# Transfers of the job's operands and sums issued by GpSimd instead of SyncE, in a hybrid decoder layer

## The chip, the cores and the metric

The kernel runs on one core of a Trainium2 chip. The metric is the device time of one launch in microseconds, lower is better. The engines are named as in the profile: PE (TensorE), DVE (VectorE), ACT (ScalarE), POOL (GpSimd) and SP (SyncE, which here only issues DMAs). Each works through its own queue in order, and an instruction that waits for a semaphore holds all that stand behind it on its engine. "SPq" in the profile is SP's queue.

## The reference

One decoder layer on x of 2048 positions by 1024 channels, all in float32:

```python
xn = rms_norm(h, ln_g)
proj = xn @ w_in                                   # 1024 -> 6144 columns
b_gate, c_gate, x_conv, g_conv, x_lru, g_lru = split(proj)
y_conv = headwise_rms_norm(b_gate * conv3(c_gate * x_conv)) * silu(g_conv)
y_lru = headwise_rms_norm(rg_lru(x_lru)) * silu(g_lru)
y = concatenate([y_conv, y_lru])                   # 2048 columns
out = rms_norm(h + y @ w_out, final_g)
```

`rg_lru` is a causal width-4 convolution, two block-diagonal gate maps with sigmoids, and a linear recurrence over the positions.

## The kernel before

Both large products run as a Strassen-Winograd scheme with seven products in place of eight. Each operand of a product is split into a high and a low float32r part, so that one product is three matmuls of 128x128 by 128x512 for each of four k blocks (`mm`, L886). One of the seven takes PE some 2.7 us.

The work is a list of 64 steps. 24 input steps for the first half of the positions (h = 0) and 24 for the second (h = 1) go in rounds of three, one round for each of the eight column blocks k: `lru` ("l"), `conv_a` ("a") and `conv_b` ("b"). 16 output steps ("o") follow. The program is written out in slots, one product each. `tick()` starts a slot: it runs what was put off with `at(slots, ...)` and then one piece of the generator `jobs()`. What a slot holds is the order of every engine's queue.

In the second half the weights' seven sums come ready from HBM (`sd`, loaded as `s<-sd` by `s_loads`, L218, seven 512 KB loads a step). SP issues such a load when PE has freed one of seven buffers.

From step 30 (h = 1, k = 2) on, `jobs()` prepares the left operand of the first six output blocks beside the input steps. One job, of which one runs in each round:

- `load_z` loads four tiles `raw` of y (from `yd`, L309) and their row factors `zr` (from `rsd`, L312 or L314 and L316) into the eight buffers of the pool `raw`. Where h = 0 each of the four `zr` tiles takes two DMAs, so a job has 12 loads, else 8. Jobs 1, 2, 5 and 6 have 12, jobs 3 and 4 have 8.
- two and three slots later DVE multiplies raw by zr, then adds and subtracts to get the seven sums (`s`, `raw`).
- for each sum ACT casts the high part (`so`, L417), DVE takes the low part, and `so` is stored (L422, 512 KB, seven for each job). Its tile is one of four of the tag "hl", which the high parts of the norms (`qh`, `ql`) and `st` use too.
- jobs 1 to 4 also take two blocks of `w_out` each: four loads `traw` (`blocks`, L381) into buffers that `zr` has left, four sums on DVE (`sums`, `more`), four stores `td` (L395).

All of these DMAs, and every other one but two, stand on SP, in the order of the program. That order also holds the stores `yd<-gl` and `yd<-gb` of each round's results (`finish`, L575), two for each, which read the tile g of `lru` or `conv_b`. These tiles share a tag with two buffers ("o2"), so the next round's first write to gl waits for the store of the one before last in that tag.

POOL makes in the second half the products g * sigmoid(g) (`silu`: gl and gb, 128x1024) and the two parts of the gate weights (`load_gate_w`: bh, bl), some 6 us a round. The DVE instruction L570 in `finish` reads these products. The kernel is built with `dynamic_dma_scratch_size=1024`; no DMA stands on POOL.

Of the kernel before, what the change touches and what calls it, by code (L numbers as in the profile page):

```python
# [17 lines left out]
P = 128  # L18
# [4 lines left out]
NB = C // P  # L23
# [15 lines left out]
def hymba_kernel(ctx: ExitStack, tc: tile.TileContext, x, xt, w_in, par, lamc, w_gate, w_out, final_g, out):  # L39
    nc = tc.nc  # L40
# [100 lines left out]
    def at(slots, *fs):  # L141
        if slots == 0:
            for f in fs:
                f()
        else:
            due.append([slots, fs])
# [150 lines left out]
    def load_z(h, m, zr, wait):  # L297
        r = [piece("raw") for _ in range(4)]
        fs = []
        for i in range(2):  # L300
            c, b = divmod(2 * m + i, NB)
            assert c < 2 or normed
            zz_, zq_ = [], []
            z2 = wt(("u", "r")[i], "zr") if zr else None
            for q in range(2):
                zz = r[2 * i + q].rearrange("p (k t) -> p k t", k=NB)
                zq = z2[:, q * C:(q + 1) * C] if zr else piece("zr")
                k0 = (1 - h) * KT + q * NB
                nc.sync.dma_start(zz, yd[c][b, :, k0:k0 + NB, :])  # L309
                zq = zq.rearrange("p (k t) -> p k t", k=NB)  # L310
                if h == 1:
                    nc.sync.dma_start(zq, rsd[c][b:b + 1, k0:k0 + NB, :].broadcast_to((P, NB, P)))  # L312
                else:
                    nc.sync.dma_start(zq[:64], rsd[c][b:b + 1, k0:k0 + NB, :].broadcast_to((64, NB, P)))  # L314
                    k0 += KT
                    nc.sync.dma_start(zq[64:], rsd[c][b:b + 1, k0:k0 + NB, :].broadcast_to((64, NB, P)))  # L316
                fs.append(lambda zz=zz, zq=zq: tt(zz, zz, zq, ALU.mult))
        if wait is not None:
            for i in range(2):
                at(max(wait + i, 1), *fs[2 * i:2 * i + 2])  # L320
        return r, fs
# [37 lines left out]
    def jobs():  # L359
        tjobs = [(t, j) for t in (2, 3) for j in range(NB)]  # L360
        for ph, m in ((0, 0), (0, 1), (1, 0), (1, 1), (0, 2), (0, 3)):
            (a11, a12, a21, a22), fs = load_z(ph, m, False, None)
            yield
            yield
            for f in fs[:2]:
                f()
            yield
            for f in fs[2:]:
                f()
            yield  # L370
            x_ = aux("s3")
            tt(x_, a11, a21, ALU.subtract)
            tt(a21, a21, a22, ALU.add)
            b = {}

            def blocks():
                if tjobs:
                    b[0] = tjobs.pop(0)
                    b[1] = [piece("traw") for _ in range(4)]
                    for p, src in zip(b[1], w_blocks(*b[0])):  # L380
                        nc.sync.dma_start(p, src)  # L381

            def sums():
                if b:
                    b11, b12, b21, b22 = b[1]
                    tt(b11, b12, b11, ALU.subtract)
                    tt(b12, b22, b12, ALU.subtract)

            def more():
                if b:  # L390
                    b11, b12, b21, b22 = b[1]
                    tt(b22, b22, b11, ALU.subtract)
                    tt(b21, b21, b22, ALU.subtract)
                    to = td[b[0]]
                    at(1, lambda: [nc.sync.dma_start(to[n], v) for n, v in enumerate((b22, b11, b12, b21))])  # L395
                    b.clear()

            blocks()
            prev = None
            nothing = lambda: None  # L400
            items = [(0, a11, lambda: tt(a11, a21, a11, ALU.subtract)), (3, x_, nothing), (2, a21, nothing),
                     (1, a11, nothing), (4, a12, lambda: tt(a12, a12, a11, ALU.subtract)),
                     (6, a22, nothing), (5, a12, nothing)]
            for n, (i, v, after) in enumerate(items):
                if prev:
                    prev()
                    prev = None
                if n in (1, 5):
                    sums()
                if n in (2, 6):  # L410
                    more()
                if n == 4:
                    blocks()
                while not may():
                    yield
                t, = hl_tile("so")
                nc.scalar.copy(t[:, 0:C], v)  # L417

                def prev(t=t, i=i, v=v, after=after, dst=so[ph, m]):
                    tt(t[:, C:2 * C], v, t[:, 0:C].bitcast(F32), ALU.subtract)  # L420
                    after()
                    at(2, lambda: nc.sync.dma_start(  # L422
                        dst[i], t.bitcast(F32).rearrange("p (h c) -> p h c", h=2)))
                    at(3, lambda: hl_done(1))

                yield
            prev()
            made.add((ph, m))
            yield
# [854 lines left out]
```

## Time and profile before

| | |
|---|---|
| median of three runs | 1422.15 us (1421.93 to 1424.15) |
| the profiled execution's own time | 1420.66 us |
| its span in the trace | 1418.5 us |
| granted TensorE clock, mean | 0.983 |
| DVE, ACT, POOL busy | 75%, 55%, 17% of the span |
| DMA, mean rate over the span | 262 GB/s |
| DMAs named by the change | 42 so stores of 512 KB, 32 traw loads and 32 td stores of 256 KB, first and last 682.7 and 1088.7 us (with the six jobs' loads) |

A line of the profile with a time in front gives start and length in us, the engine, the line of the kernel, the operation, "written tile <- read tiles", shapes, how many in a row, and in brackets how long the engine stood still just before and what ended that. A line of the waits gives the engine and what waited, for whom, then total us, how many, and the longest. A line of a group gives after the bar the busy total and the mean in ns, and then the idle time before. Lines with three numbers between slashes are least, median and most.

### The profile page before, as it was taken

To read this page: it belongs to the slowest core of one execution; us is meant where nothing else is said; L and a number is where in the kernel's file an instruction comes from. 1 tells how busy PE (TensorE), PEld (TensorE's weight loads), DVE (VectorE), ACT (ScalarE), POOL (GpSimd) and SP (SyncE) were. 2 spreads that over 40 slices of the span, in tenths; PEclk is the share of its full clock that TensorE was granted. 3 is DMA by queue.
4 is the path that set the end of the run, shared out by engine and by line. 5 is a ranking of instruction groups with operands and counts; after the bars stand their busy time and mean duration, and the time that the engine had idled before them with its cause. 6 is when DMAs were issued, how large, how long until landed. Compare 5 with 4: busy or idle time off the path is not lost.

```text
span 1418.5 us, 16980 instructions
## 1 busy us (share of the span) xinstructions
PE 1332.1 (94%) x5732; PEld 1069.0 (75%) x5732; DVE 1070.9 (75%) x1273; ACT 782.1 (55%) x1165; POOL 245.8 (17%) x159
## 2 busy tenths in 40 slices
PE   6889999999999997899998999999996999989997
PEld 5768777778777775677886878787875788867886
DVE  7689788898989889777767667665657648668885
ACT  7576757667656756475563645463647313334443
POOL 2104333433534330001000010101010000000000
PEclk9989999999999998999999999999998999999999
DMA  5037797998888865631899999998888998698643
GB/s 213 30 118 277 266 286 213 305 321 284 312 283 297 310 244 203 235 102 30 281 318 340 330 345 331 353 301 308 277 282 318 353 298 272 207 405 298 214 155 144
DMA packets 165190, 371.02 MB, mean 262 GB/s; under 512 B 17264, under 2 KB 52464, under 8 KB 165104
## 3 DMA queue, kind: packets, MB, share of 16 engines
q1 hardware_dynamic: 164816, 369.63, 76.3%
q8 instruction: 45, 0.74, 0.2%
q14 instruction: 41, 0.34, 0.1%
q10 hardware_dynamic: 288, 0.32, 0.1%
HBM read 224.45 MB, written 145.43 MB: 261 GB/s over the span
## 4 chain that ended last, share of the span: by engine, by line
PE 64%; DMA 12%; ACT 10%; DVE 8%; issue 3%; SPq 1%; POOL 0%; DVEq 0%; ACTq 0%
PE bank L886 61%; ACT i L673 2%; DMA traw<-in_w_out_dram 2%; ACT r L673 2%; PE norm_ps L559 2%; PE gate L666 2%; DVE s L160 2%; DMA zr<-rsd 2%; DMA raw<-yd 1%; DMA s<-so 1%; DVE traw L160 1%; DMA yd<-gl 1%; DVE tl L160 1%; DMA sd<-s 1%; DMA traw<-td 1%
## 5 line engine op out<-in xcount | busy, mean ns | idle before, releaser
L886 PE MATMUL bank<-th,s 128*128 128x512 f32 x3608 | 1143.7, 393 | 44.6 <-DMA s<-so 8.8
L886 PEld LDWEIGHTS bank<-th,s 128*128 128x128 f32 x3608 | 683.4, 189 | 206.4 <-issue 11.0
L886 PE MATMUL bank<-tl,s 128*128 128x512 f32 x1804 | 709.1, 393 | 7.5 <-DVE tl L160 7.3
L886 PEld LDWEIGHTS bank<-tl,s 128*128 128x128 f32 x1804 | 341.6, 189 | 82.5 <-DVE tl L160 11.6
L160 POOL TENSOR_TENSOR s<-raw,s 128x512 fp32r<-128x512 f32 x62 | 120.8, 1961 | 252.3 <-ACT s L197 177.3
L197 ACT CAST s<-raw 128x512 fp32r<-128x512 f32 x136 | 81.9, 616 | 58.9 <-PE bank L886 46.0
L1223 ACT COPY u<-bank 128x512 f32<-128x512 f32 x58 | 34.0, 586 | 139.1 <-PE bank L886 90.1
L160 DVE TENSOR_TENSOR tl<-traw,th 128x512 fp32r<-128x512 f32 x102 | 69.4, 706 | 48.8 <-ACT th L454 29.4
L160 DVE TENSOR_TENSOR s<-s,s 128x512 fp32r<-128x512 f32 x102 | 99.9, 980 | 5.4 <-ACT s L197 5.4
L160 POOL TENSOR_TENSOR gb<-gb,sg 128x1024 f32<-128x1024 f32 x16 | 42.2, 2634 | 352.0 <-ACT sg L599 259.5
L160 DVE TENSOR_TENSOR s<-raw,s 128x512 fp32r<-128x512 f32 (+1 forms) x120 | 93.4, 802 | 10.0 <-ACT s L197 5.3
L1220 ACT COPY q<-bank 128x512 f32<-128x512 f32 x58 | 33.8, 583 | 82.2 <-PE bank L886 77.1
L160 DVE TENSOR_TENSOR raw<-raw,zr 128x512 f32<-128x512 f32 x64 | 50.0, 804 | 33.4 <-DMA zr<-rsd 33.3
L197 ACT CAST s<-s 128x512 fp32r<-128x512 f32 x102 | 62.9, 616 | 4.6 <-DVE s L160 4.5
L640 DVE SCALAR_TENSOR_TENSOR u<-xl,pt,u 128x1024 f32<-128x1024 f32 x48 | 63.6, 1326 | 0.8 <-ACT u L636 0.2
L1226 ACT COPY rr<-bank 128x512 f32<-128x512 f32 x58 | 33.9, 584 | 45.9 <-PE bank L886 45.8
L750 DVE SCALAR_TENSOR_TENSOR t<-p,pt,t 128x1024 f32<-128x1024 f32 x32 | 47.6, 1487 | 6.1 <-ACT t L747 5.4
L160 DVE TENSOR_TENSOR st<-u,st 64x1024 fp32r<-64x1024 f32 x32 | 50.4, 1575 | 1.0
L160 POOL TENSOR_TENSOR gl<-gl,sg 128x1024 f32<-128x1024 f32 x16 | 44.7, 2793 | 16.9 <-ACT sg L599 16.9
L160 DVE TENSOR_TENSOR ob<-bank,rr 128x512 f32<-128x512 f32 x18 | 12.2, 689 | 44.8 <-ACT rr L1226 44.8
L636 ACT ACTIVATE u<-xl,pt 128x1024 f32<-128x1024 f32 x16 | 19.9, 1245 | 46.5 <-DVE xl L160 46.4
L729 ACT COPY p<-bank 128x512 f32<-128x512 f32 x17 | 10.0, 586 | 62.7 <-PE bank L886 60.0
(162 smaller groups left out, 1395.4 us busy)
## 6 DMA issues: line engine op xcount, KB each, us to landing
sd<-s SPq DMA_DIRECT2D x147, 512.0 KB, 4.9
s<-sd SPq DMA_DIRECT2D x147, 512.0 KB, 6.2
raw<-in_w_in_dram SPq DMA_DIRECT2D x108, 256.0 KB, 5.1
so<-so SPq DMA_DIRECT2D x42, 512.0 KB, 6.2
s<-so SPq DMA_DIRECT2D x42, 512.0 KB, 7.5
raw<-yd SPq DMA_DIRECT2D x64, 256.0 KB, 5.7
traw<-in_w_out_dram SPq DMA_DIRECT2D x56, 256.0 KB, 5.9
yd<-gl SPq DMA_DIRECT2D x32, 256.0 KB, 3.7
```

What stands on the lines that cost most here:

```text
L160: (eng or nc.vector).tensor_tensor(out=out, in0=a, in1=b, op=op)
L197: nc.scalar.copy(dst[i][0], val(i))
L559: nc.tensor.matmul(norm_ps[0], sel[:, s0:s0 + R], q[:, i * C:(i + 1) * C], start=norm_ps[1] == 0, stop=norm_ps[1] == 8 * KT - 1)
L636: nc.scalar.activation(out=v["u"], in_=o1[:, 1:1 + N2], func=AF.Identity, scale=lw[0], bias=pt[:, LB + k:LB + k + 1])
L640: nc.vector.scalar_tensor_tensor(out=v["u"], in0=o1[:, 1 + j:1 + j + N2], scalar=lw[j], in1=v["u"], op0=ALU.mult, op1=ALU.add)
L666: nc.tensor.matmul(ps[j], v["gw"][n][:, j, :], v["st"][j][:, sl], start=(n == 0), stop=(n == 1))
L673: nc.scalar.activation(out=g_[hi, sl], in_=v["ps"][j][src], func=AF.Sigmoid, bias=pt[src, bias + k:bias + k + 1])
L750: nc.vector.scalar_tensor_tensor(out=tcur["t"], in0=p[:, 2 + j:2 + j + N2], scalar=cw[j], in1=tcur["t"], op0=ALU.mult, op1=ALU.add)
L886: nc.tensor.matmul(bank, a[:, js], b, start=start and n == 0, stop=stop and n == 2, skip_group_check=more)
L1220: nc.scalar.copy(q1, bk["A"])
L1223: nc.scalar.copy(u2, bk["A"])
L1226: nc.scalar.copy(rr, bk["A"])
```

## The change

Four places issue from `nc.gpsimd` in place of `nc.sync`: `load_z` when it is called by `jobs()` (`zr` false; the output steps' own calls stay on SP), the `traw` loads, the `td` stores and the `so` stores. Sizes, tiles and the order on PE, DVE and ACT stay as they are.

```diff
-                nc.sync.dma_start(zz, yd[c][b, :, k0:k0 + NB, :])
+                (nc.sync if zr else nc.gpsimd).dma_start(zz, yd[c][b, :, k0:k0 + NB, :])
...
-                    nc.sync.dma_start(zq, rsd[c][b:b + 1, k0:k0 + NB, :].broadcast_to((P, NB, P)))
+                    (nc.sync if zr else nc.gpsimd).dma_start(zq, rsd[c][b:b + 1, k0:k0 + NB, :].broadcast_to((P, NB, P)))
...
-                    nc.sync.dma_start(zq[:64], rsd[c][b:b + 1, k0:k0 + NB, :].broadcast_to((64, NB, P)))
+                    (nc.sync if zr else nc.gpsimd).dma_start(zq[:64], rsd[c][b:b + 1, k0:k0 + NB, :].broadcast_to((64, NB, P)))
                     k0 += KT
-                    nc.sync.dma_start(zq[64:], rsd[c][b:b + 1, k0:k0 + NB, :].broadcast_to((64, NB, P)))
+                    (nc.sync if zr else nc.gpsimd).dma_start(zq[64:], rsd[c][b:b + 1, k0:k0 + NB, :].broadcast_to((64, NB, P)))
...
-                        nc.sync.dma_start(p, src)
+                        nc.gpsimd.dma_start(p, src)
...
-                    at(1, lambda: [nc.sync.dma_start(to[n], v) for n, v in enumerate((b22, b11, b12, b21))])
+                    at(1, lambda: [nc.gpsimd.dma_start(to[n], v) for n, v in enumerate((b22, b11, b12, b21))])
...
-                    at(2, lambda: nc.sync.dma_start(
+                    at(2, lambda: nc.gpsimd.dma_start(
                         dst[i], t.bitcast(F32).rearrange("p (h c) -> p h c", h=2)))
```

SP's queue before, in round 3 (job 3, eight loads), from the last pair of the job's loads on; `sd_108` and `sd_109` are the sums of two steps, `yd_86` and `yd_87` the two halves of the stored gl:

```order
L309 DMA raw<-yd_84 128x512
L312 DMA zr<-rsd_88 128x512
L218 DMA s<-sd_108 128x1024
L422 DMA so_121<-so 128x1024
L218 DMA s<-sd_108 128x1024
L218 DMA s<-sd_109 128x1024 x2
L575 DMA yd_86<-gl 128x4x128
L575 DMA yd_87<-gl 128x4x128
L381 DMA traw<-in_w_out_dram 128x512 x4
```

The same place of SP's queue with the change:

```order
L218 DMA s<-sd_107 128x1024 x7
L218 DMA s<-sd_108 128x1024 x7
L218 DMA s<-sd_109 128x1024 x2
L575 DMA yd_86<-gl 128x4x128
L575 DMA yd_87<-gl 128x4x128
L218 DMA s<-sd_109 128x1024 x4
```

The job's loads, sums' stores and weight blocks have left it; between the s<-sd loads and the gl stores nothing else is left.

POOL's queue at that place before, from the gl product of one round to that of the next:

```order
L160 TENSOR_TENSOR gl<-gl,sg 128x1024
L160 TENSOR_TENSOR gb<-gb,sg 128x1024
L615 TENSOR_SCALAR bh<-bd 128x256
L616 TENSOR_TENSOR bl<-bd,bh 128x256
L160 TENSOR_TENSOR gl<-gl,sg 128x1024
```

and with the change, from the same last pair of loads (four td, one so and three more such pairs stand ahead of it) to the next gl product:

```order
L309 DMA raw<-yd_84 128x512
L312 DMA zr<-rsd_88 128x512
L422 DMA so_121<-so 128x1024
L381 DMA traw<-in_w_out_dram 128x512 x4
L160 TENSOR_TENSOR gb<-gb,sg 128x1024
L422 DMA so_124<-so 128x1024
L395 DMA td_132<-traw 128x512 x4
L422 DMA so_124<-so 128x1024
L615 TENSOR_SCALAR bh<-bd 128x256
L616 TENSOR_TENSOR bl<-bd,bh 128x256
L160 TENSOR_TENSOR gl<-gl,sg 128x1024
```

The gb product now stands behind the job's loads and the four traw loads, and the gate weights' parts behind the td stores.

## The prediction

> **What bounds the kernel now.** I read the busy times first, then a table of equal stretches, then the waits of PE there, then the queues' own order in time. The page's first part says that PE is the bound:
>
> ```profile
> PE 1332.1 (94%) x5732; PEld 1069.0 (75%) x5732; DVE 1070.9 (75%) x1273; ACT 782.1 (55%) x1165; POOL 245.8 (17%) x159
> ```
>
> So only time in which PE stands still can be won: 1418.5 - 1332.1 = 86 us in all. The changed transfers run from 682 to about 1089 us, and one round of three steps takes some 65.8 us there. The table of stretches, cut into such rounds (length; busy us of PE, PEld, DVE, ACT, POOL with their counts; granted clock, DMA share, GB/s):
>
> ```profile
> 671.50:737.20 65.70, 65.52 (x289) 53.37 (x288) 44.60 (x47) 35.17 (x46) 6.13 (x4) 1.00 0.88 297
> 737.20:803.00 65.80, 61.26 (x265) 48.64 (x264) 44.65 (x51) 32.41 (x44) 5.92 (x4) 1.00 0.99 335
> 803.00:868.80 65.80, 62.18 (x270) 49.69 (x269) 44.92 (x52) 33.55 (x45) 6.48 (x4) 1.00 0.97 337
> 868.80:934.50 65.70, 61.98 (x270) 49.49 (x269) 45.09 (x52) 33.34 (x45) 5.91 (x4) 1.00 0.97 336
> 934.50:1000.20 65.70, 62.04 (x263) 49.40 (x262) 39.64 (x47) 32.66 (x43) 7.81 (x4) 0.97 0.85 286
> 1000.20:1066.00 65.80, 65.62 (x288) 53.24 (x287) 41.88 (x47) 36.37 (x50) 7.39 (x4) 1.00 0.85 285
> ```
>
> Each round holds one job, 1 to 6. In rounds 1 and 6 PE idles 0.2 us; in rounds 2 to 5 it idles 4.5, 3.6, 3.7 and 3.7, that is 4.3 + 3.4 + 3.5 + 3.5 = **14.7 us** above an undisturbed round. This is the ceiling of what the change can win there. The waits of PE from 700 to 1000 us add up to the same:
>
> ```profile
> PE bank L886 <- DMA s<-sd: 5.6, 5, 2.5
> PE norm_ps L559 <- DVE ql L160: 5.0, 4, 1.4
> PE bank L886 <- ACT q L1220: 4.2, 3, 1.4
> ```
>
> What lies behind them is in the queues in order of time, round 2, first SP's, then DVE's:
>
> ```profile
> 744.49 1.92 SPq L395 DMA_DIRECT2D td<-traw  x4
> ...
> 748.27 0.45 SPq L309 DMA_DIRECT2D raw<-yd  x1
> ...
> 757.00 0.45 SPq L316 DMA_DIRECT2D zr<-rsd  x1
> ...
> 761.28 1.12 SPq L575 DMA_DIRECT2D yd<-gl  x2
> ```
>
> ```profile
> 762.39 0.69 DVE L160 TENSOR_TENSOR raw<-raw,zr 128x512 f32<-128x512 f32 x1 [1.28 <-DMA zr<-rsd]
> ...
> 769.91 0.69 DVE L160 TENSOR_TENSOR gl<-bank,rr 128x512 f32<-128x512 f32 x1 [5.49 <-DMA yd<-gl]
> ```
>
> SP spends 748.27 to 757.45 on a job's twelve loads (four of 256 KB, eight of 128 KB: 2 MB). The store of the finished gl is issued only at 761.28, behind them, and lands when DVE's wait ends, over 8 us later. DVE may not write the next gl into that buffer before, so it stands for 5.49 us; ql, xl and the bank copies behind it come late, and PE waits for ql and q. The s<-sd loads queued behind the twelve are late too, hence the third wait. The same wait of DVE for yd<-gl ends at 835.57, 901.35 and 969.98 in rounds 3 to 5 (rows below).
>
> **What goes away.** SP loses 17 issues of such a round ahead of the gl store (four td, one so, twelve loads; thirteen where the loads are eight), and the store is no longer behind their bytes. It may then issue as soon as gl is ready and PE has freed the buffers of the s<-sd loads ahead of it, and lies behind s<-sd alone. It needs to land 4.3 us sooner in round 2 and 3.4 or 3.5 in the others; the twelve issues alone held SP for 9.2 us. So I take the store as no longer last. **What is late next** is the job's own data: the same DVE queue multiplies raw by zr just ahead of gl, and these loads are now POOL's.
>
> **What is added.** POOL issues the same DMAs, in the order td, so, loads. It is nearly empty there (6 of 65.8 us busy), so the sum depends on one unknown, the price p of one issue on POOL, which this trace doesn't show. The nearest rows:
>
> ```profile
> L422 SPq DMA_DIRECT2D so<-so x42: 319/383/870, 705.0 to 1088.7; - x42
> L616 POOL TENSOR_TENSOR bl<-bd,bh 128x256 fp32r<-128x256 f32 x16 | 16.5, 1034 | 1.3
> L160 POOL TENSOR_TENSOR gb<-gb,sg 128x1024 f32<-128x1024 f32 x16 | 42.2, 2634 | 352.0 <-ACT sg L599 259.5 <-DMA raw<-yd 72.5 <-DVE xcol L520 20.0
> ```
>
> Low end: SP's own 0.38 us for the same DMA; an issue cannot cost less than nothing, and no row gives a reason for less than SP. High end: 2.63 us, a POOL pass over a whole 128x1024 tile. I take **p = 1.0 us**, the price of POOL's own small pass (1.03), as an issue is an instruction of that engine that touches little data. The Trainium skill's page "DMA: Bandwidth & Descriptors" (Specifications) gives about 1 us to the first byte from GpSimd and about 0.6 from Sync. No run here shows POOL's; by that ratio an estimate from SP's row would be 0.64 us, and the sum would be the full 14.7.
>
> How late may the data be? After the last multiply DVE has 2.0 us of work (762.39 to 764.4) ahead of gl. PE stays undisturbed if gl starts at 769.91 - 4.3 = 765.6, so round 2 has 1.2 us to spare. The other rounds, DVE then SP:
>
> ```profile
> 828.41 0.68 DVE L160 TENSOR_TENSOR s<-raw 128x512 f32<-128x512 f32 x1
> 835.57 0.69 DVE L160 TENSOR_TENSOR gl<-bank,rr 128x512 f32<-128x512 f32 x1 [5.75 <-DMA yd<-gl]
> 893.11 0.69 DVE L160 TENSOR_TENSOR raw<-raw,zr 128x512 f32<-128x512 f32 x1
> 901.35 0.69 DVE L160 TENSOR_TENSOR gl<-bank,rr 128x512 f32<-128x512 f32 x1 [6.22 <-DMA yd<-gl]
> 961.03 0.69 DVE L160 TENSOR_TENSOR raw<-raw,zr 128x512 f32<-128x512 f32 x1 [1.20 <-DMA zr<-rsd]
> 969.98 0.69 DVE L160 TENSOR_TENSOR gl<-bank,rr 128x512 f32<-128x512 f32 x1 [6.93 <-DMA yd<-gl]
> ```
>
> ```profile
> 811.31 1.90 SPq L395 DMA_DIRECT2D td<-traw  x4
> 820.90 0.32 SPq L312 DMA_DIRECT2D zr<-rsd  x1
> 876.98 1.76 SPq L395 DMA_DIRECT2D td<-traw  x4
> 886.25 0.32 SPq L312 DMA_DIRECT2D zr<-rsd  x1
> 942.75 2.00 SPq L395 DMA_DIRECT2D td<-traw  x4
> 956.55 0.45 SPq L316 DMA_DIRECT2D zr<-rsd  x1
> ```
>
> Likewise the spare is 2.4 us in round 3 (828.41 is one multiply, 0.69, past the last start, so ready at 829.8 against 832.2), 2.7 in round 4 (895.1 against 897.85) and 3.5 in round 5 (963.0 against 966.5). From the first td issue to the end of the last load SP took 13.0, 9.9, 9.6 and 14.25 us for 17, 13, 13 and 17 issues. POOL can start at the same moment, since the td stores wait for DVE's traw sums, and needs 17p or 13p. At p = 1.0 the loads come 4.0, 3.1, 3.4 and 2.75 us later, past the spare by 2.8, 0.7, 0.7 and 0, so the rounds win 1.5 + 2.7 + 2.8 + 3.5 = **10.5 us**. Above 1.04 us each round loses, and the sum is 71.25 - 60p: nothing is left at **p = 1.19**, 6.8 us are lost at 1.3 and 18.8 at 1.5. At 0.85 or less nearly all 14.7 are won.
>
> Two smaller terms of unlike sign remain. The raw<-yd loads land a median 5.7 us after issue, 2.9 at least (first row below); in a queue of POOL's own with one issue a microsecond they may land up to 2.8 us sooner (gain up to that for each round that is past its spare). Against it, the four traw loads now follow the last multiply and the last so store on POOL: they end about 1.8 us later than SP's (762.49 to 766.75, below), while DVE comes 1.5 to 2.8 us earlier to the sums that read them; a wait of up to 2.5 us in rounds 2 to 4.
>
> ```profile
> DMA to landing us min/median/max: 2.9/5.7/10.3
> 762.49 4.26 SPq L381 DMA_DIRECT2D traw<-in_w_out_dram  x4
> 776.84 1.28 DVE L570 SCALAR_TENSOR_TENSOR gb<-t,pt,gb 128x1024 f32<-128x1024 f32 x1
> ```
>
> I let the two nearly cancel and keep 9 us. The gate weights' pass and the gb product now stand behind DMAs on POOL. In round 2 the gb product would end near 770.5 (last load 761.5, so, four traw held to 768.1, then 2.4 of its own), and its reader on DVE starts at 776.84 today: hidden, and with that cover gone it would cost DVE what it lacks. Rounds 1 and 6 idle 0.2 us now and have nothing to win; in round 1 nothing of a job stands ahead of the loads on POOL, so they can go early. The last so stores (to 1088.7) leave SP during the change to the output steps; I count that as nothing, since the next steps' loads queue on SP as before.
>
> **Rivals.** *POOL issues too slowly* (slower). If one issue takes over 1.23 us, the sum falls below -2.8 us; 1.5 gives 1422 + 19 = 1441. For it: 17 issues in a row with DVE standing right behind. Against it: POOL's small pass is shorter, and POOL has some 60 us of a round free. The Trainium skill's page "SBUF — State Buffer" (Who interferes with whom) says that GpSimd cannot write its DMA descriptors while VectorE runs certain two-port instructions, though not tensor_tensor. The DVE rows above are tensor_tensor and scalar_tensor_tensor, and no row here shows such a hold. As a mechanism of this kernel it is the same price: DVE is busy 44.65 us of round 2, and half a pass (0.69 to 1.28 us) on top of each issue makes p about 1.5.
>
> *The DMA engines are the bound.* Their share is 0.99, 0.97, 0.97 and 0.85 in rounds 2 to 5, so if a round cannot pass a share of 1.00, it shortens by at most 0.7, 2.0, 2.0 and 3.5 us, 8.2 together. Then no load lands sooner either, and the traw wait counts, say half of 2.5 us in three rounds: 8.2 - 3.8 = 4.4, so 1418. For it: GB/s over share is near 340 in all six rounds. Against it, the output steps move more at the same share:
>
> ```profile
> 1250.00:1300.00 50.00, 40.93 (x172) 32.63 (x171) 34.94 (x52) 21.02 (x38) 0.00 (x0) 0.97 1.00 376
> ```
>
> The page "DMA: Bandwidth & Descriptors" of the Trainium skill (Issuing engines are not separate DMA queues) holds that issuing from more engines saves only issue time. By it the whole gain is in the issue gaps and the order, as counted here.
>
> *A wait takes the place of the one removed* (no change). DVE waits for its multiply's data as long as it did for gl's store, or ACT for the so store, which stays behind the loads; this is p near 1.19: 0 us, 1422.
>
> **How the numbers follow.** The profiled execution took 1420.66 us, its span 1418.5; it lies 1.5 us under the median of the three runs, 1422.15, and I apply the difference to the median: 1422.15 - 9 = 1413. The chances: forecast (p under about 1.1) 0.46, DMA engines 0.12, a wait in its place 0.17, POOL too slow 0.25. A change of 0.2%, 2.8 us, is about what a measurement can tell from none. Faster is the first two, 0.58. The range begins at the full 14.7 and rounding, 1406, and reaches to p = 1.38, 1434; the dearer end up to 2.63 us (1422 + 87) is left out, with some 0.15.
>
> **What would show it.** Right: DVE's wait for yd<-gl nearly gone from rounds 2 to 5, PE busy above 64 us a round, SP no longer waiting for DVE at td, so and traw, POOL's issues near 1 us each. Wrong: DVE waiting longer than now for raw and zr, or at all for traw; ACT's so casts waiting longer for the so stores; gb's reader on DVE waiting for POOL; or rounds as long as before at a DMA share of 1.

## The result and the profile after

The forecast was 1413 us; the change made the kernel slightly slower, by 0.4%.

| | before | after |
|---|---|---|
| median of 19 runs each | 1420.3 us | 1426.84 us |
| ratio, 95% interval | | 1.0043 [1.0035, 1.0052] |
| profiled execution, and its span | 1420.66, 1418.5 us | 1424.25, 1422.5 us |
| PE busy, PE idle (span less busy) | 1332.1, 86.4 us | 1336.8, 85.7 us |

The profiled execution of the change is one of the faster of its 19, so the two traces account for 4.0 us, and 2 to 3 us of the difference between the medians are in no trace.

Busy times of the page first, then the table of stretches for rounds 2 to 5, with the columns of the one before the change:

```profile
PE 1336.8 (94%) x5732; PEld 1073.5 (75%) x5732; DVE 1070.0 (75%) x1273; ACT 781.9 (55%) x1165; POOL 340.6 (24%) x329
```

```profile
737.20:803.00 65.80, 60.77 (x259) 48.65 (x258) 43.39 (x50) 31.74 (x42) 25.87 (x39) 0.97 0.93 328
803.00:868.80 65.80, 61.20 (x267) 49.17 (x266) 44.80 (x52) 33.34 (x44) 23.58 (x35) 1.00 0.93 337
868.80:934.50 65.70, 62.86 (x268) 50.54 (x267) 45.42 (x51) 33.22 (x44) 23.35 (x36) 0.97 0.92 337
934.50:1000.20 65.70, 62.02 (x262) 49.81 (x260) 40.84 (x45) 31.67 (x43) 19.29 (x27) 0.95 0.83 283
```

PE stands in rounds 2 to 5 about as much as before (16.15 us in sum, 15.54 before), and the granted clock is below 1.00 in three of them, not in one: over the whole span PE's busy time is 4.7 us longer for the same 5732 matmuls. The waits from 680 to 1060 us, of PE, DVE and ACT:

```profile
PE norm_ps L559 <- DVE ql L160: 14.1, 4, 4.8
PE bank L886 <- ACT q L1220: 1.4, 1, 1.4
...
DVE raw L160 <- DMA zr<-rsd: 45.5, 18, 5.2
...
DVE gl L160 <- DMA yd<-gl: 4.8, 3, 3.9
...
ACT so L417 <- DMA so<-so: 33.8, 5, 8.8
```

The wait that was to go has gone: DVE waited 27.6 us for `yd<-gl` before, 4.8 now, and PE waits for `s<-sd` no more. In their place DVE waits 45.5 us for the job's data (19.9 before), and PE's three kinds of short wait have become one long wait a round, for ql. POOL's queue and DVE's in round 2, in order of time, show why:

```profile
747.79 0.54 POOL L309 DMA_DIRECT2D raw<-yd  x1
...
750.26 0.52 POOL L316 DMA_DIRECT2D zr<-rsd  x1 [1.39 <-issue]
750.90 0.58 POOL L309 DMA_DIRECT2D raw<-yd  x1
...
761.10 0.52 POOL L316 DMA_DIRECT2D zr<-rsd  x1 [1.83 <-DMA raw<-yd]
...
768.04 0.54 POOL L381 DMA_DIRECT2D traw<-in_w_out_dram  x1 [1.09 <-DVE raw L160]
768.59 2.35 POOL L160 TENSOR_TENSOR gb<-gb,sg 128x1024 f32<-128x1024 f32 x1
```

```profile
750.14 2.35 DVE L700 TENSOR_TENSOR_SCAN r<-r,hl,u 128x1024 f32<-128x1024 f32 x1
...
766.90 0.69 DVE L160 TENSOR_TENSOR raw<-raw,zr 128x512 f32<-128x512 f32 x1 [0.90 <-DMA zr<-rsd]
...
768.23 3.27 DVE L160 TENSOR_TENSOR raw<-raw 128x512 f32<-128x512 f32 x1
771.43 0.68 DVE L160 TENSOR_TENSOR gl<-bank,rr 128x512 f32<-128x512 f32 x1
```

Three things are to be seen. An issue on POOL takes 0.54 us, half of the 1.0 us that the prediction took, and yet the twelve loads take from 747.79 to 761.62, since seven of them wait. The last waits for the landing of the load eight issues ahead of it; the chain of work that ended last, in order of time, goes through both (the second number is the length of each piece in us):

```profile
750.90 9.74 DMA raw<-yd
760.63 0.47 issue
761.10 5.68 DMA zr<-rsd
```

The gb product stands behind the traw loads, which wait for DVE's multiplies, and starts at 768.59. And DVE's `raw<-raw`, 0.69 us elsewhere, takes 3.27 beside that product, just ahead of gl, which starts at 771.43.

This collision is not new; its place is. Before, the gb product ran from 757.55 to 759.96 and slowed one of two multiplies, which together took 2.92 us (two such passes take 1.41 elsewhere):

```profile
758.19 2.92 DVE L160 TENSOR_TENSOR raw<-raw,zr 128x512 f32<-128x512 f32 x2 [1.46 <-DMA zr<-rsd]
```

There it cost nothing, because DVE then still waited 1.28 us for its next data and 5.49 us for the store.

**One number tells each round:** how long after the scan (L700) DVE's first write to the next gl starts: 771.43 - 750.14 = 21.3 us here, 769.91 - 750.02 = 19.9 before. Set against the time from this scan to the next, from the same rows of each round:

| gl after the scan / length of the round, us | round 2 | 3 | 4 | 5 |
|---|---|---|---|---|
| before | 19.9 / 66.8 | 18.7 / 65.7 | 18.8 / 65.8 | 21.7 / 65.8 |
| after | 21.3 / 68.2 | 19.5 / 66.4 | 19.1 / 66.0 | 20.0 / 66.2 |
| e1, loads alone on POOL | 17.6 / 64.6 | 16.1 / 63.0 | 16.9 / 63.8 | 18.3 / 62.4 |
| e2, so and td alone | 18.6 / 65.6 | 18.4 / 65.4 | 18.8 / 65.7 | 18.3 / 62.5 |
| e9, loads and so | 19.6 / 66.6 | 17.9 / 64.9 | 18.3 / 65.2 | 20.1 / 64.3 |
| e8, loads and traw | 19.4 / 66.3 | 17.6 / 64.6 | 18.7 / 65.6 | 18.5 / 62.6 |
| e6, all but traw | 20.3 / 67.3 | 18.4 / 65.4 | 17.2 / 64.2 | 20.1 / 66.5 |
| e7, gb ahead of traw | 19.3 / 71.0 | 18.7 / 67.7 | 18.7 / 65.7 | 20.0 / 65.4 |
| e12, half of s<-sd | 18.2 / 65.1 | 17.6 / 64.6 | 17.5 / 64.4 | 16.8 / 60.9 |

In rounds 2 to 4 the length is gl's start plus 46.9 to 47.0 us in every kernel of the table but e7; in round 5 it is never less than gl's start plus 44.1. So in this table a round is as long as gl is late. What exceeds the sum has other causes, shown below: late traw loads in rounds 2 and 3 of e7, and in round 5 of the change a stretch of PE at half clock. In round 5 of e6 and e7 such a stretch follows too, after waits of PE of 3.67 and 3.61 us, but there its price was not tested.

### The profile page after: what moved, and what is told of

Its sections match the earlier page's. It is cut to its first block, busy times and chain, and to the rows that moved or that the text cites. A ratio compares the mean times of both kernels' runs of the same rounds, so it can differ in the third digit from the quotient of the medians.

```text
span 1422.5 us, 17003 instructions
## 1 busy us (share of the span) xinstructions
PE 1336.8 (94%) x5732; PEld 1073.5 (75%) x5732; DVE 1070.0 (75%) x1273; ACT 781.9 (55%) x1165; POOL 340.6 (24%) x329
## 3 DMA queue, kind: packets, MB, share of 16 engines
q1 hardware_dynamic: 142384, 318.24, 65.4%
## 4 chain that ended last, share of the span: by engine, by line
PE 64%; DVE 11%; DMA 10%; ACT 9%; issue 5%; POOL 1%; SPq 0%; DVEq 0%; ACTq 0%; POOLq 0%
PE bank L886 60%; ACT i L673 2%; ACT r L673 2%; PE norm_ps L559 2%; DMA sd<-s 2%; DMA zr<-rsd 2%; DMA yd<-gl 2%; PE gate L666 2%; DVE s L160 2%; DMA s<-so 2%; DMA traw<-in_w_out_dram 1%; DVE r L700 1%; DVE tl L160 1%; DVE traw L160 1%; DVE u L160 1%
## 5 line engine op out<-in xcount | busy, mean ns | idle before, releaser
L160 DVE TENSOR_TENSOR raw<-raw,zr 128x512 f32<-128x512 f32 x64 | 44.5, 717 | 56.5 <-DMA zr<-rsd 56.5
L640 DVE SCALAR_TENSOR_TENSOR u<-xl,pt,u 128x1024 f32<-128x1024 f32 x48 | 65.7, 1370 | 0.8 <-ACT u L636 0.2
L422 POOL DMA_DIRECT2D so<-so x42 | 23.2, 552 | 170.3 <-DVE so L160 128.2
L454 ACT CAST th<-traw 128x512 fp32r<-128x512 f32 x56 | 32.9, 619 | 26.3 <-DMA traw<-in_w_out_dram 12.9
L160 DVE TENSOR_TENSOR st<-u,st 64x1024 fp32r<-64x1024 f32 x32 | 46.1, 1442 | 1.0
```

The lines of the kernel that those rows point to most:

```text
L160: (eng or nc.vector).tensor_tensor(out=out, in0=a, in1=b, op=op)
L454: nc.scalar.copy(self.dst[i, j][0], self.r[i, j])
L640: nc.vector.scalar_tensor_tensor(out=v["u"], in0=o1[:, 1 + j:1 + j + N2], scalar=lw[j], in1=v["u"], op0=ALU.mult, op1=ALU.add)
```

## The experiments

Rounds below are those of the table. Three theories were named as the runs went on. A: two queues share the engines, so that the loads on POOL, which have no slack, now land beside SP's s<-sd loads, which have some. B: POOL's queue has room for few DMAs in flight, and its loads stand behind stores. C: transfers issued by POOL are slow by themselves. D and K come with their runs.

### Parts of the change alone

**e1**, only the loads of `load_z` on POOL:

```diff
-                        nc.gpsimd.dma_start(p, src)
+                        nc.sync.dma_start(p, src)
...
-                    at(1, lambda: [nc.gpsimd.dma_start(to[n], v) for n, v in enumerate((b22, b11, b12, b21))])
+                    at(1, lambda: [nc.sync.dma_start(to[n], v) for n, v in enumerate((b22, b11, b12, b21))])
...
-                    at(2, lambda: nc.gpsimd.dma_start(
+                    at(2, lambda: nc.sync.dma_start(
```

> Only the jobs' raw and zr loads go on POOL; td, so and traw stay on SP. Theory A (the loads, once in a queue of their own, share the DMA engines with the s<-sd loads that used to stand behind them in SP's one queue): the loads still land in 8 to 10 us in rounds 2 to 5 (before: about 6), DVE waits 35 us or more for zr in all, and the time is no better than with the whole change: 1422 to 1430. Theory B (too little room in flight on POOL: seven or eight transfers, of which td and so take five ahead of the loads): the loads now find that room empty, their last issue comes about 4 us sooner than with the whole change, PE's waits for ql halve, and the time is 1412 to 1418, under before's 1420. Theory C (a transfer issued by POOL is slow by itself): as A for the landing, whatever else moves.

1412.08 us, ratio 0.9936 [0.9918, 0.9955] to before: faster than both kernels, and at the low end of B's range. Its DVE in round 2:

```profile
755.66 0.68 DVE L160 TENSOR_TENSOR raw<-raw,zr 128x512 f32<-128x512 f32 x1
...
766.90 0.69 DVE L160 TENSOR_TENSOR raw<-raw,zr 128x512 f32<-128x512 f32 x1 [3.36 <-DMA s<-sd]
...
768.23 0.69 DVE L160 TENSOR_TENSOR raw<-raw 128x512 f32<-128x512 f32 x1
769.24 0.69 DVE L160 TENSOR_TENSOR gl<-bank,rr 128x512 f32<-128x512 f32 x1 [0.31 <-DMA yd<-gl]
```

With no store ahead of them the loads are all issued by 755.7 (the first at 728.96), the gb product runs at 759.16, and `raw<-raw` is short. This is against A as the main cause, and the median landings, 7.0 to 7.9 us, are below A's 8 to 10. (The trace names `s<-sd` as what the last multiply waited for; that multiply does not read s, so the name is doubtful.) But the last multiply starts 15.3 us after the scan (at 751.62), later than before (762.39 - 750.02 = 12.4): with the loads on a second queue the data do come later.

**e2**, only the so and td stores on POOL; **e9**, loads and so; **e8**, loads and traw; **e6**, loads, so and td (each the change with the other places back on `nc.sync`).

> Only the so and td stores go on POOL; raw, zr and traw stay on SP. A: the burst of loads keeps SP's queue to itself with the s<-sd loads behind it, so it lands in about 6 us as before and starts some 2 us earlier, as five issues ahead of it are gone: 1412 to 1419. B: the same, as POOL then holds at most five transfers at once. C: the so stores land later than before's 6.2 us and ACT's so casts wait longer than before's 19 us in all, which eats the gain: 1419 to 1424.

> Only the job's loads and the so stores on POOL; traw and td on SP. Theory B: the loads stand behind an so store that waits for DVE and go 10 us later than with the loads alone (1412 there): 1418 to 1424. Theory D: the gb product stands behind the last load and one so store, not behind traw, and runs before raw<-raw: 1411 to 1416.

> Only the job's loads and the traw loads on POOL; td and so stores on SP. The loads can go as early as with the loads alone on POOL (1412 there). Theory B: 1410 to 1415, as no store stands ahead of the loads. Theory D: the gb product is again behind the traw loads, which wait for the multiplies, so it runs beside raw<-raw: 5 to 12 us above the loads alone, 1417 to 1424.

> The change with the traw loads left on SP; loads, td and so stores on POOL. Theory D: nothing that waits for DVE's multiplies stands ahead of the gb product any more, so it runs some 4 us sooner, beside multiplies that wait for data anyway: 1414 to 1419. Theory B: the loads still stand behind td and so on POOL and wait for room: 1424 to 1428.

| on POOL | median us | ratio to before |
|---|---|---|
| loads (e1) | 1412.08 | 0.9936 [0.9918, 0.9955] |
| so, td (e2) | 1416.27 | 0.9962 [0.9949, 0.9976] |
| loads, traw (e8) | 1418.51 | 0.9979 [0.9969, 0.9990] |
| loads, so (e9) | 1418.81 | 0.9986 [0.9975, 0.9997] |
| loads, so, td (e6) | 1419.62 | 0.9993 [0.9980, 1.0006] |
| all (the change) | 1426.84 | 1.0043 [1.0035, 1.0052] |

The loads alone gain, and so do the so and td stores alone; whatever joins the loads costs them 6 us or more. The traw loads cost some 6 us when they join the loads (e8 against e1) and some 7 when they join all the rest (the change against e6).

- e2 came out as A and B had it (1412 to 1419), below C's 1419 to 1424.
- e8 came out as D had it (1417 to 1424), and it has the collision back in rounds 2 to 4: `raw<-raw` takes 3.28, 3.29 and 3.29 us there.
- e6 lies just above D's 1414 to 1419 and below B's 1424 to 1428. With traw back on SP the gb product starts at 762.40 in round 2, and `raw<-raw` takes 0.69 us again.
- e9's time is the one that B had (1418 to 1424), but B's reason does not show: its data come at most 0.8 us later than e1's (table below), and what holds gl is the store again. DVE waits for `yd<-gl` 8.8 us in rounds 2 to 5 of e9, 1.3 in e1.

How late the data are, as the start of the last multiply after the scan:

| last multiply after the scan, us | round 2 | 3 | 4 | 5 |
|---|---|---|---|---|
| before | 12.4 | 11.0 | 10.6 | 12.7 |
| e1, loads alone on POOL | 15.3 | 13.4 | 13.9 | 15.8 |
| e8, loads and traw | 14.8 | 12.7 | 14.0 | 16.4 |
| e9, loads and so | 16.1 | 13.1 | 13.5 | 16.4 |
| e6, all but traw | 16.9 | 14.7 | 14.8 | 18.2 |
| the change | 16.8 | 14.9 | 14.6 | 17.8 |
| e12, half of s<-sd | 13.6 | 11.8 | 12.9 | 14.3 |

With the loads alone on POOL the data come 2.4 to 3.3 us later than before. Adding so or traw alone moves them by at most 0.8 us; with so and td both ahead of the loads (e6, the change) they come 3.8 to 5.4 us later than before.

### More room for POOL's queue

**e4**, the change with `dynamic_dma_scratch_size` 1280 in place of 1024:

> The changed kernel with dynamic_dma_scratch_size 1280 in place of 1024, nothing else. The waits marked issue ahead of the third load, when seven POOL transfers are in flight, would end if that size sets how many may be in flight (64 entries of 16 bytes for each DMA engine, nine of them a transfer, so seven; 80 entries, so eight). A: the marked waits may go, but the loads land as late as before, so the time stays within 2 us of the changed kernel's 1427. B: one more in flight of seven takes 1 us or so off each burst: 1421 to 1425. C: unchanged.

1426.87 us, ratio 1.0043 [1.0024, 1.0061]: no difference. The waits named "issue" ahead of the loads fell (L309 from 4.8 us to 0.3), but the waits for earlier landings stayed, so the ring alone is not the limit. A's and C's forms of the expectation came out, B's 1421 to 1425 did not.

### The gl store alone on POOL

**e3**, before, with the second half's `yd<-gl` stores issued by POOL.

> The kernel before, with only the two yd<-gl stores of each round of the second half on POOL; all that the change moved stays on SP. If the store's place behind the burst in SP's queue is what PE waits for in the kernel before (my reading of its profile, which the change did not test since the loads got late too): the store leaves as soon as gl is ready, near 754 in round 2 in place of 761, shares the DMA engines with the burst and lands by 762 or so, DVE's wait of 27.6 us for yd<-gl falls below 8, PE idles at most 1.5 us a round in place of 3.6 to 4.5, and the time is 1406 to 1413. By C the store lands late enough (9 us or more) that a third of the wait stays: 1413 to 1417. If the DMA engines' rate is the bound, the rounds keep 65 us: 1418 to 1421.

1424.57 us, ratio 1.0020 [1.0007, 1.0032]; every expectation missed. POOL and DVE in round 3:

```profile
822.58 0.81 POOL L575 DMA_DIRECT2D yd<-gl  x1 [31.89 <-DVE gl L570]
830.13 0.76 POOL L575 DMA_DIRECT2D yd<-gl  x1 [6.74 <-issue]
830.90 2.42 POOL L160 TENSOR_TENSOR gb<-gb,sg 128x1024 f32<-128x1024 f32 x1
```

```profile
830.69 3.18 DVE L160 TENSOR_TENSOR raw<-raw 128x512 f32<-128x512 f32 x1
837.17 0.69 DVE L160 TENSOR_TENSOR gl<-bank,rr 128x512 f32<-128x512 f32 x1 [3.30 <-DMA yd<-gl]
```

The second half of the store waits 6.74 us with nothing else of POOL's shown in flight but the first half, then holds the gb product back until it meets `raw<-raw`, as in the change. What it waits for the trace does not name ("issue"). The stores themselves landed a median 6.4 us after issue (8.1 from SP before), so that a transfer issued by POOL is slow by itself, theory C, is not seen here.

### The collision taken out

**e7**, the change with the gb product one slot earlier, ahead of the four traw loads in POOL's queue. D: the product, pushed behind DMA issues, runs beside DVE's `raw<-raw`, and this makes the loss.

```diff
-    def silu(g, late=0):
+    def silu(g, late=0, slot=4):
...
-        at(4 + late, lambda: tt(g, g, sg[0], ALU.mult, nc.gpsimd))
+        at(slot + late, lambda: tt(g, g, sg[0], ALU.mult, nc.gpsimd))
...
-                silu(g)
+                silu(g, 0, 3 if h else 4)
```

> The change with one swap on POOL: the gb product stands ahead of the four traw loads instead of behind them, in rounds 2 to 5; everything else as in the change. Theory D (the product, pushed behind DMA issues, runs beside DVE's raw<-raw just ahead of gl: 3.27 us instead of 0.69 in rounds 2 to 4, and the long wait of PE for ql that this makes is followed by a stretch at half clock): raw<-raw is back at 0.69, gl starts some 2.5 us sooner in three rounds, PE's waits for ql fall to 2.5 us or less, and the clock stays up: 1414 to 1419. Theory B (the loads come late on POOL, because issues wait for room or stand behind stores): the loads are as late as in the change, 1425 to 1428.

1425.82 us, ratio 1.0033 [1.0021, 1.0045]: as B had it. `raw<-raw` is back at 0.69 in all rounds (in rounds 2 and 5 the product now slows a multiply ahead of it), and gl starts 1.95, 0.74 and 0.40 us sooner in rounds 2 to 4, not 2.5. In rounds 3 and 4 this is because it now waits 1.6 us for `yd<-gl`. In rounds 2 and 3 even that is lost, and more; but the profiled execution, 1430.51 us, was the slowest of the 12, so these losses may be above the usual. DVE, ACT and PE in round 2:

```profile
773.70 0.69 DVE L160 TENSOR_TENSOR traw<-traw 128x512 f32<-128x512 f32 x1 [1.15 <-DMA traw<-in_w_out_dram]
776.53 0.69 DVE L160 TENSOR_TENSOR traw<-traw 128x512 f32<-128x512 f32 x1 [2.13 <-DMA traw<-in_w_out_dram]
777.14 0.68 DVE L160 TENSOR_TENSOR xl<-bank,q 128x512 f32<-128x512 f32 x1
...
777.92 1.24 ACT L636 ACTIVATE u<-xl,pt 128x1024 f32<-128x1024 f32 x1 [5.85 <-DVE xl L160]
779.07 0.56 ACT L1220 COPY q<-bank 128x512 f32<-128x512 f32 x1
...
779.68 0.79 PE L886 MATMUL bank<-th,s 128*128 128x512 f32 x1 [3.16 <-ACT q L1220]
```

The traw loads are later than DVE's sums by 3.28 us, xl stands behind these sums, ACT behind xl, and PE behind ACT's copy q. So D is real as a step but not the cause of the whole: behind the collision stand the store, then traw. Held against e6, which gained some 7 us, the cost lies in the traw loads' place on POOL: there they either hold the gb product back or come late themselves.

### PE kept busy in its long wait

**e11**, the change with twelve matmuls by a zero part of `sel` between the qh and the ql matmuls of gl's norm. K: a long wait of PE is followed by a stretch at half clock.

```diff
                 norm_ps[1] += 1
+                if h == 1 and i == 0 and q is qh and KT + 3 <= row <= KT + 6:
+                    for _ in range(12):
+                        nc.tensor.matmul(norm_ps[0], sel[:, 0:R], qh[:, 0:C], start=False, stop=False)
```

> The change, with twelve more matmuls of PE in each of rounds 2 to 5, by a zero part of sel, so that the sums stay as they are; they stand between the qh and the ql matmuls of gl's norm, where PE waits for ql, and take some 2.7 us of each wait. Theory K (a wait of PE of some 3 us or more in one piece is followed by a stretch at half clock, which costs the change 5 us against before): the waits for ql fall to 2 us or less, the half-clock stretches of rounds 2 to 5 go (13.7 us in the change, that is 6.8 us lost), and the time falls to 1418 to 1422 although the work is more. Rival (the clock has another cause, or the late data alone make the time): the same stretches, 1426 to 1429.

1424.84 us, ratio 1.0024 [1.0010, 1.0038]. By its k the edit fell on rounds 3 to 6, so round 2 is the control. Stretches of 4 us of both kernels (columns as above; the clock is the last but two), first of the change in rounds 4 and 5, then with PE filled, in rounds 2, 4 and 5:

```profile
908.00:912.00 4.00, 4.00 (x16) 3.01 (x15) 3.96 (x7) 1.72 (x3) 1.28 (x3) 0.80 0.52 206
972.00:976.00 4.00, 3.43 (x8) 2.49 (x9) 3.96 (x6) 1.46 (x2) 1.13 (x2) 0.50 0.72 282
```

```profile
776.00:780.00 4.00, 4.00 (x12) 3.09 (x11) 3.92 (x7) 1.71 (x2) 0.95 (x3) 0.52 0.45 176
908.00:912.00 4.00, 3.35 (x15) 2.39 (x13) 3.93 (x7) 0.98 (x1) 0.59 (x1) 1.00 0.82 323
972.00:976.00 4.00, 2.65 (x13) 1.36 (x12) 3.93 (x7) 1.10 (x2) 0.00 (x0) 1.00 0.97 391
```

Where the wait was filled the clock stays at 1.00; in round 2, unfilled, PE waited 6.1 us and the clock fell to half. K's link is shown. Its price is less than K had: round 5 is gl's start plus 46.2 us in the change and plus 44.1 here, so 2.1 us, while round 4 is gl's start plus 46.9 in both. The whole time fell by some 2 us, not by 5: it lies between K's 1418 to 1422 and the rival's 1426 to 1429, and the interval overlaps the change's a little.

### What makes the data late

**e12**, the change with the s<-sd loads of steps 31 to 47 halved.

```diff
-            nc.sync.dma_start(tile_.bitcast(F32), src[i])
+            nc.sync.dma_start(tile_.bitcast(F32)[:, 0:w, :], src[i][:, 0:w, :])
+            dst[i] = (tile_[:, 0, :], tile_[:, w - 1, :])
```

> The change, with the s<-sd loads of steps 31 to 47 cut to their first half (256 KB in place of 512 KB; the low part of s is left out, and the products with it read the high part). Theory A (sharing): the job's loads on POOL land in 5 to 7.5 us instead of 8.4 to 10.2, and the last multiply of round 2 starts some 13 to 14.5 us after the scan L700 instead of 16.8; 1412 to 1420. Theories B and C (room on POOL's queue, or transfers of POOL slow by themselves): landing stays at 8 us or more, the last multiply at 16 or later; 1421 to 1428.

1412.83 us, ratio 0.9934 [0.9911, 0.9958]. The last multiply of round 2 starts 13.6 us after the scan instead of 16.8, the median landings of the four load lines are 7.1 to 8.2 us instead of 8.4 to 10.2, DMA share 0.78 instead of 0.93. The collision is still there (`raw<-raw` 3.32, 3.29 and 3.29 us in rounds 2 to 4). The time and the multiply answer to A; the landings lie between A's and the others' numbers. So with half the bytes of s<-sd beside the burst its data come 1.7 to 3.5 us a round sooner. That this is sharing alone is not shown: the so and td stores land sooner too (medians 4.2 and 2.9 us instead of 5.3 and 4.3), which makes room in POOL's queue sooner, and the kernel before with half of s<-sd was not run.

**e10**, the loads issued by ACT, everything else as before (`nc.scalar` in place of `nc.gpsimd` in `load_z`, the rest on `nc.sync`).

> The job's loads issued by ACT, everything else on SP as before. Theory A (two queues with work share the engines, whatever issues them, so a burst beside SP's s<-sd loads lands later than one in SP's own queue): its loads land a median 7 to 9 us after issue, as from POOL, and the last multiply starts 14 to 17 us after the scan L700 in rounds 2 to 5 (before: 12.4 in round 2). Theory C (transfers issued by POOL are slow by themselves): they land as from SP, 5.5 to 6.5 us, and the last multiply starts at 11 to 12.5. Time: the gl store goes early in both; ACT gives the issues 2 to 5 us just ahead of the copy q, so 1408 to 1420 by C and 1412 to 1424 by A.

1458.11 us, ratio 1.0245 [1.0222, 1.0269]. Its issues waited for earlier landings too, and ACT's copies behind them:

```profile
769.20 0.45 ACTq L316 DMA_DIRECT2D zr<-rsd  x1
769.69 0.59 ACT L1220 COPY q<-bank 128x512 f32<-128x512 f32 x1 [14.01 <-DMA zr<-rsd]
```

That cost far more than either theory allowed, and it spoils the comparison: the loads landed a median 6.5 to 7.4 us after issue, between the two. The last multiply, 13.4 to 15.7 us after the scan in rounds 2 to 5, is nearer to A's 14 to 17 than to C's 11 to 12.5. C is not excluded by it, but the stores speak against a large part of C: from POOL the so and td stores landed in a median 5.3 and 4.3 us in the change, and in 6.4 and 5.4 in e2, against 5.9 and 4.0 from SP before.

### Is it the store or the data?

**e13** is before, **e14** is e7 and **e15** is e1, each without the second half's `yd<-gl` stores of four column blocks (the first half's values are stored in their place, earlier). By their k these are the stores of rounds 3 to 6, not 2 to 5.

```diff
-                nc.sync.dma_start(yd[2 * h + i][:, :, kt, :].rearrange("b p t -> p b t"),
-                                  sil[:, i * C:(i + 1) * C].rearrange("p (b t) -> p b t", b=NB))
+                for j in ((0, 2) if h == 0 else ()) if KT + 3 <= kt <= KT + 6 else (2 * h,):
+                    nc.sync.dma_start(yd[j + i][:, :, kt, :].rearrange("b p t -> p b t"),
+                                      sil[:, i * C:(i + 1) * C].rearrange("p (b t) -> p b t", b=NB))
```

> The kernel before, without the stores yd<-gl of rounds 2 to 5; the first half's values are stored in their place, in the first half, so four blocks of the second half hold the first half's y. Theory P (the landing of that store is what holds gl there, as the prediction has it): gl starts as soon as the job's data are summed, some 14.5, 13, 12.7 and 14.8 us after the scan L700 in rounds 2 to 5 (19.9, 18.7, 18.8, 21.7 with the store), PE idles 1 us or less a round, and 12 to 15 us go: 1406 to 1410. Rival (another wait takes its place at once): gl at 16 or later, 1413 to 1420.

> The change with gb ahead of traw (as in the run of that name, 1425.8), without the stores yd<-gl of rounds 2 to 5, their values taken from the first half as above. If the job's data hold gl there: gl at some 19, 17, 17 and 20 us after the scan, 1417 to 1423, and it stays well above the kernel before without these stores. If the store's landing is the main thing in the change too: gl at 16 or sooner, 1406 to 1414.

> Only the job's loads on POOL (1412 with the stores), without the stores yd<-gl of rounds 2 to 5, their values taken from the first half. The last multiplies start 15.3, 13.4, 13.9 and 15.8 us after the scan there, so if the data hold gl it starts 0.3 to 1 us sooner than with the store, and the time is 1409 to 1412. If sharing the engines is what delays the data, 512 KB less a round bring the multiplies 1 to 1.5 us forward: 1406 to 1409.

| gl after the scan / length of the round, us | round 2 (store kept) | 3 | 4 | 5 | median us, ratio to before |
|---|---|---|---|---|---|
| e13, before | 20.5 / 67.4 | 12.9 / 63.6 | 12.3 / 62.6 | 13.7 / 62.0 | 1414.18, 0.9954 [0.9940, 0.9968] |
| e14, e7 | 19.2 / 71.4 | 18.4 / 68.6 | 18.0 / 68.5 | 22.3 / 68.6 | 1434.46, 1.0104 [1.0086, 1.0122] |
| e15, e1 | 17.7 / 65.1 | 15.8 / 62.8 | 16.3 / 63.3 | 17.8 / 62.0 | 1410.61, 0.9926 [0.9913, 0.9939] |

DVE in round 4, of e13 and then of e14:

```profile
883.01 2.35 DVE L701 TENSOR_TENSOR_SCAN r<-r,hl,u 128x1024 f32<-128x1024 f32 x1
...
891.39 2.72 DVE L160 TENSOR_TENSOR raw<-raw,zr 128x512 f32<-128x512 f32 x2 [1.04 <-DMA zr<-rsd]
...
895.35 0.68 DVE L160 TENSOR_TENSOR gl<-bank,rr 128x512 f32<-128x512 f32 x1
```

```profile
891.02 2.35 DVE L701 TENSOR_TENSOR_SCAN r<-r,hl,u 128x1024 f32<-128x1024 f32 x1
...
907.10 0.69 DVE L160 TENSOR_TENSOR raw<-raw,zr 128x512 f32<-128x512 f32 x1 [2.25 <-DMA zr<-rsd]
...
909.03 0.68 DVE L160 TENSOR_TENSOR gl<-bank,rr 128x512 f32<-128x512 f32 x1
```

In the kernel before, the store is the whole wait: without it gl starts 12.3 us after the scan, straight behind the data, as theory P had it. The total missed P's 1406 to 1410 and lies in the rival's 1413 to 1420. In part this is because round 2 kept its store; and the rounds are now 48.3 to 50.7 us longer than gl's start, so at 62 to 64 us another limit takes over, which the runs do not name. In e7's form of the change the store hardly matters: gl is 18.0 us after the scan without it, straight behind data that come some 6 us later. The total missed both ranges (1417 to 1423 and 1406 to 1414). The waits that grew are the one seen in e7, PE for q, 11.7 us in all from 680 to 1060 us, and ACT's casts for so stores, 43.4 us (33.8 in the change); that they make the time is read from the trace and was not tested. e15 came out as expected where the data hold gl (1409 to 1412). Its last multiplies started 13.9, 14.3 and 15.9 us after the scan in rounds 3 to 5, no sooner than e1's: 512 KB less a round did not bring the data forward by the 1 to 1.5 us that sharing was to give.

## Why the prediction was wrong, step by step

**The ceiling was about right.** The store's landing bounds the rounds before; taking it away in rounds 3 to 5 shortened them by 2.1, 3.2 and 3.8 us (e13 against before), where the prediction had 3.4, 3.5 and 3.5.

**The price p was mis-sized, and it was not the question.** A POOL issue took 0.54 us, not 1.0. By the prediction's own formula nearly all 14.7 us should have been won. (The measured time fits the formula at p near 1.27 and lies in the range; that is luck.) The formula had the loads late by their count times p; they were late by waiting. In round 2 the burst ended 4.2 us later than on SP (761.62 against 757.45), close to the 4.0 predicted, but for another reason: the issues waited for room behind the td and so stores and for earlier landings, and landings took a median 8.4 to 10.2 us, not 5.6 to 6.6. The prediction had even counted on landings up to 2.8 us sooner in a queue of POOL's own. Half of s<-sd taken away brought the data of round 2 3.2 us forward (e12).

Waits for an earlier landing stood on SP before, too, where the prediction counted the burst's 9.2 us as issues alone: 1.7 us of them were such waits (on POOL 7.3 of 13.8). And in the chain of the kernel before, the issue of the gl store itself follows the landing of the raw load issued eight DMAs ahead of it:

```profile
755.40 5.81 DMA raw<-yd
...
761.28 0.56 SPq L575
...
761.89 7.89 DMA yd<-gl
```

So on either queue a load that lands late also holds back what is issued behind it, and on POOL this outweighed p.

**"The store is no longer last" failed in part.** It was issued at 755.00 instead of 761.28, but the DMA view from 747 to 767 us gives its landing, before and then after:

```profile
yd<-gl SPq DMA_DIRECT2D x2, 256.0 KB, 7.9
```

```profile
q0 software_dynamic: 1252, 4.02, 62.8%
q1 hardware_dynamic: 1456, 2.57, 40.7%
...
s<-sd SPq DMA_DIRECT2D x7, 512.0 KB, 12.7
...
yd<-gl SPq DMA_DIRECT2D x2, 256.0 KB, 14.3
```

The 6.3 us won at the issue were given back by a landing 6.4 us longer: the engines move no more bytes (337 GB/s in round 3, as before), and POOL's queue takes the larger part of them. The Trainium skill's page "DMA: Bandwidth & Descriptors" (Issuing engines are not separate DMA queues) holds that issuing from more engines saves only issue time. The shared engines agree with it; the prediction read it as a gain without a cost, and these rows show the cost, in who is served first. In rounds 3 and 4 of e7, where the collision is off gl's path, gl waits for the store again.

**"Hidden" failed for the gb product.** The prediction had it end near 770.5 and looked only at its reader; it ended at 770.94, but it ran beside DVE's `raw<-raw`, on the path. That cost 3.27 - 0.69 = 2.6 us in each of rounds 2 to 4. The Trainium skill's page "SBUF — State Buffer" (Who interferes with whom) has this rule: a VectorE instruction with two SBUF inputs contends with a GpSimd instruction that reads SBUF, and one of them blocks. These rows agree, 3.27 us against 0.69. The prediction drew on that section for descriptor writes alone and passed this over.

**The sum.** By the prediction's lateness, gl was to start 18.4, 16.1, 16.0 and 18.2 us after the scan in rounds 2 to 5 (its latest undisturbed start in each, plus what the loads pass the spare by). It started at 21.3, 19.5, 19.1 and 20.0: 11.2 us later in sum, 7.8 of it the collision and the rest, 3.4, the data, whose lateness was predicted as 4.0, 3.1, 3.4 and 2.75 us and came out as 4.4, 4.0, 4.0 and 5.1. With 2.1 us of half clock in round 5 and 1.2 us in round 6 (scan to scan 74.9 us, 73.7 before) this turns -10.5 into +4.0, which is what the spans differ by. It is an account of one trace against another, not a list of what each cause would give back alone: with the collision off its path (e7) the store and the traw loads took its place, and the median fell by 1 us.

**The two small terms did not cancel.** The landing relief did not come; the traw wait is hidden in the change, since gl is late anyway, and appears as soon as gl is not (e7). The so stores did wait behind the loads as the third rival said: ACT's wait for them rose from 19.1 to 33.8 us (680 to 1110 us).

**What was not foreseen** is the clock: the change gathers several waits of PE into one of 2.7 to 4.9 us a round.

**The signs named.** Gone as predicted: DVE's wait for `yd<-gl` (nearly), SP's waits for DVE at td, so and traw. Came as warned: longer waits for zr, longer waits of ACT for so. PE above 64 us a round did not come. The rival nearest to the result is a wait that takes the place of the one removed, though not through p.

**Left open:** how the lateness of the data in the change divides between sharing, the waits for room and earlier landings in POOL's queue, and a small part of C. Most of it, 2.4 to 3.3 us a round, comes with the loads alone (e1), the rest only with so and td both ahead of them (e6 against e9), and none with a longer ring (e4). e12 shows that the bytes of s<-sd matter, but not by which way; e15 shows that the gl store's bytes do not.

## What to carry to other kernels

Moving transfers to a second queue does not only save issue time: it takes away an order. Before, the burst stood ahead of most of the s<-sd loads in SP's queue and landed in 5.6 to 6.6 us; after, both were in flight together, and it landed in 8.4 to 10.2. Move the transfers that have nothing waiting ahead of them in the new queue (the loads alone won 0.6%), and ask of each compute instruction on that engine what it now stands behind and what it will run beside.

## What the runs showed of the hardware that was not expected

- A POOL DMA issue took 0.52 to 0.62 us for these shapes in the change, a median 0.78 for the store in 512-byte pieces (e3).
- Issues waited when seven or eight DMAs of their queue were in flight: on POOL 1.39 us at 750.26 with seven, and 1.83 at 761.10 for the landing of the DMA eight ahead; on SP before, the gl store at 761.28 in the same way. A larger ring did not change the time. In e3, with 512-byte pieces, POOL waited 6.74 us with one of its DMAs in flight, for a reason that the trace does not name.
- Where a DVE pass of 128x512 and a POOL product of 128x1024 met, one of the two was slowed: the pass took 3.27 to 3.28 us in place of 0.69 in rounds 2 to 4 of the change, while in round 2 of e1 the pass kept 0.69 and the product took 2.89 in place of 2.4.
- A single wait of PE was followed by a stretch at half clock each time that it was 3.5 us or longer (4.85 and 3.57 us in rounds 2 and 5 of the change, 6.14 in round 2 of e11). Shorter ones went both ways: 2.66 us in round 4 of the change was followed by one, and even 2.01 in round 3 of e6 (granted clock 0.50 from 840 to 842 us), while 3.03 in round 3 of the change was not. Where matmuls filled the wait, the clock stayed at 1.00.
